# Single transposes and another order in the memory stage of an encoder block

## The chip, the cores and the metric

The kernel runs on one core of one Trainium2 chip. The metric is the device time of one execution in microseconds (us), and the time before is the median of three runs. The core has a matrix engine (TensorE: PE for its products, PEld for its weight loads), a vector engine (DVE), a scalar engine (ACT), GpSimd (POOL), and a sync engine (SP) that issues transfers here. Each engine works through its own list of instructions in order and waits for the others by semaphores.

## The reference

One layer of a residual block on 256 rows (T) of 1024 columns (D), in float32:

```python
x = x + 0.5 * rmsnorm(swiglu(rmsnorm(x), ffn1_w_in, ffn1_w_down))       # FFN 1, width 2816
h = rmsnorm(x)
q_a, f_a, i_a, g_a, q_b, k_b, v_b, f_b, gates = split(h @ w_in)
o_a = rmsnorm(hgrn2(q_a, f_a, i_a)) * silu(g_a)                         # gated recurrence, 8 heads
o_b = fox_attention(q_b, k_b, v_b, f_b)                                 # causal attention, 8 heads
y = sigmoid(gate_a) * (o_a @ w_branch_a) + sigmoid(gate_b) * (o_b @ w_branch_b)
x = x + rmsnorm(y @ w_out)
# the memory stage: 4 heads of 256, 256 rows of memory
q = rmsnorm(x) @ w_mq
k, v = split(rmsnorm(mem) @ w_mkv)
x = x + rmsnorm((softmax(q @ k.T / 16) @ v) @ w_mo)
x = x + 0.5 * rmsnorm(swiglu(rmsnorm(x), ffn2_w_in, ffn2_w_down))       # FFN 2
```

All norms have gains of their own.

## The kernel before

**Numbers as pairs.** Every float32 operand of a product is held as a high part (rounded to the float32r format by an ACT copy) and a low part (what is left, by a DVE subtraction). `split` makes such a pair, `gain_split` makes it with a norm's gain multiplied in, `Pair` holds one for a transposed 1024 x 256 activation. A product of two pairs is three TensorE products: high by high, high by low, low by high.

**Weights.** `unit` brings one weight block of 128 x 1024 (512 KB, 260 in all): a transfer to `raw`, the ACT copy to `hi` (L119) and the DVE subtraction to `lo` (L120). There are buffers for four raw blocks and eight pairs. `chunk` is four units.

**Two kinds of projection.** `proj_tok` has the activations stationary and 512 weight columns moving: rows on partitions in the result. `proj_col` has the weights stationary and 256 rows moving: a transposed result. Each takes eight contraction blocks (kb) of three products.

**Halves and transposes.** The 256 rows are worked on as two halves h of 128. After each sublayer `post` takes the norm of a half from the accumulators (two squares on ACT, a chain of small DVE steps for the reciprocal root, `rstd_of`) and adds it to the residual `xs` (L296, two instructions of 512 columns). Then `half` transposes that half for the next sublayer: `to_T` issues eight TensorE transposes of 128 x 128, four to a bank of `trp` (two banks), and a `gain_split` of each block into X1 to X4. `half` also starts the next reciprocal root, r1 to r4. In the FFN that begins with its first columns row by row (FFN 2: `n_tok` = 2), `act_T` transposes 128 x 256 activations in pairs.

**Order of the work.** The instructions are written down in program order, and a planner with a cost model puts each engine's list into order: of what it takes to be ready, the earliest in the program goes first. The list of products is kept in `log`. `after(i)` gives the instructions inside it high priority, and those on TensorE may not stand ahead of product `log[i]`. This is a lower bound: if the planner takes the operands to be ready later, they stand later. The constants say how many products after a mark (`m`, `n`, or before the end of `log` for `L_OA`): `L_F1` for X2's first half, counted from the last products of FFN 1; `L_IA` for X2's second half, in the projection `i_a`; `L_OA` for OA, the recurrence's output; `L_WO` and `L_MK` for X3 (the memory stage's queries); `L_MO` and `L_F2` for X4 (FFN 2); `L_ACT` and `L_ACT2` for `act_T`.

**The memory stage (L796 to L904).** `rows_proj` with `w_out` ends in accumulators `po[h]`. In program order there follow keys (`mk`, two chunks, 96 products each of 256 columns), queries (`mq`, the same, from X3), values 0 (`mem_v(0)`, 48 products of 512 columns), then for each half the scores (24 products of 256 columns) and the softmax (a maximum per head on DVE, four exponentials on ACT, the normalization L863) and eight transposes of p (L867) with their splits into `pT`; then values 1, and `mem_out(0)` to `mem_out(3)`, 12 products of 256 columns for each of the four heads, which need `pT` and the values, and whose results in the `trp` banks are split into AO; last the projection `mo` from AO.

Of the kernel before, what the change touches and what calls it, by code (L numbers as in the profile page):

```python
# [16 lines left out]
P = 128  # L17
D = 1024
T = 256
# [9 lines left out]

L_ACT = 15  # L30
L_ACT2 = 27
L_F1 = 18
L_IA = 22
L_WO = 18
L_MK = 46
L_MO = 18
L_F2 = 44
L_OA = 20
F_T = (10, 50)
F_O = (30, 75)  # L40
M_O = (24, 36)

R_AT = (12, 30, 48, 68, 88, 120, 160, 193, 218)

# [19 lines left out]
def block_kernel(ctx: ExitStack, tc: tile.TileContext, wts, x_in, xT_in, mem_in, memT_in, cols, rows, fbias, masks, out):  # L64
# [193 lines left out]
    def gain_split(X, kb, src, g, a=0, b=T):  # L258
        gs = cols_s[:, g + kb : g + kb + 1]
        S.activation(X.hi(kb, a, b), src, AF.Copy, scale=gs)  # L260
        V.scalar_tensor_tensor(out=X.lo(kb, a, b), in0=src, scalar=gs, in1=X.hi(kb, a, b).bitcast(F32), op0=ALU.mult, op1=ALU.subtract)  # L261

    def to_T(X, src, h, g):

        for q in range(2):
            ps = trp()
            for j in range(4):
                kb = 4 * q + j
                PE.transpose(ps[:, j * P : (j + 1) * P], src(kb), ident)  # L269
# [31 lines left out]
    def ffn(w_in, w_dn, X, r2, row, n_tok, i_row, first_half, second_half=None):  # L301
        acts = {}

        def scale_row(z, ps):
            if isinstance(ps, list):
                for i in range(2):
                    V.tensor_tensor(out=z[:, i], in0=ps[i], in1=row, op=ALU.mult)
            else:
                V.tensor_tensor(out=z, in0=ps, in1=bc(row, [P, 2, T], 1), op=ALU.mult)  # L309

        def act_tok(c, h):
            ps = mm()
# [4 lines left out]
            V.scalar_tensor_tensor(out=a, in0=ps[:, FC:], scalar=r2[h], in1=sg, op0=ALU.mult, op1=ALU.mult)  # L317
            return a

        def act_T(a, h, act):  # L320
            tr = trp()
            for j in range(2):
                PE.transpose(tr[:, j * P : (j + 1) * P], a[:, j * P : (j + 1) * P], ident)
            split(act[:, 0, :, h * P : (h + 1) * P], act[:, 1, :, h * P : (h + 1) * P], tr[:, :FC].rearrange("p (j t) -> p j t", j=2))

        def act_col(c, act, first=None):
            u = chunk(w_in, c)
            if first:
                pg, pu = proj_first(X, u, first)
            else:  # L330
                pg = proj_col2(X, u, (0, 1))
            z = m4([P, 2, 2, T], n="z")
            scale_row(z[:, 0], pg)
            S.activation(z[:, 0], z[:, 0], AF.Silu)  # L334
            if not first:
                pu = proj_col2(X, u, (2, 3))
            scale_row(z[:, 1], pu)
            V.tensor_tensor(out=z[:, 0], in0=z[:, 0], in1=z[:, 1], op=ALU.mult)
            split(act[:, 0], act[:, 1], z[:, 0])

        def down(c, h):
            act = acts[c]
            hs = slice(h * P, (h + 1) * P)
            for j in range(2):
                wh, wl = unit(w_dn, 2 * c + j)
                ah, al = act[:, 0, j, hs], act[:, 1, j, hs]
                for n in range(2):
                    ns = slice(n * 512, (n + 1) * 512)
                    for i, (a, w) in enumerate(((ah, wh), (ah, wl), (al, wh))):
                        MM(accs[h][n], a, w[:, ns], start=(c == 0 and j == 0 and i == 0), stop=(c == NFF - 1 and j == 1 and i == 2))  # L350

        late = None
        for c in range(n_tok):
            acts[c] = m4([P, 2, 2, T], F32R, "act")
        for h in range(2):
            m = len(log)
            for c in range(n_tok):
                n = len(log)
                ev = act_tok(c, h)
                if late:  # L360
                    with after(n + L_ACT):
                        late()
                late = (lambda ev=ev, c=c, h=h: act_T(ev, h, acts[c]))
            if h == 0 and n_tok:
                second_half(m)
        accs = None
        done = 0
        if callable(row):
            row = row()
        for c in range(n_tok, NFF):  # L370
            acts[c] = m4([P, 2, 2, T], F32R, "act")
            n = len(log)
            act_col(c, acts[c], {0: [acc] * 4, 1: [mm, mm, trp, trp]}.get(c))
            if late:
                with after(n + L_ACT2):
                    late()
# [50 lines left out]

    def half(X, r, h, g, m):

        with after(m):  # L430
            to_T(X, x_blocks(h), h, g)
        r[h] = rstd_x(x_halves(h))

    ffn("f1_in", "f1_dn", X1, r1, row1, 0, 0, lambda m: half(X2, r2, 0, G_MIX, m + L_F1))
# [294 lines left out]
            S.activation(t[:, h, :], ps, AF.Copy, scale=r2[h])  # L729
        vb_.append(t)  # L730
    for h in range(2):
        with after(len(log) - L_OA * (2 - h)):
            to_T(OA, lambda kb: Gt[kb // 4][:, h, (kb % 4) * P : (kb % 4 + 1) * P], h, G_HG)


    zs = []
# [75 lines left out]
    for c in range(2):  # L812
        u = chunk("mk", c)
        KM.more()
        for j in range(2):
            js = slice(2 * j, 2 * j + 2)
            ps = proj_col2(M, u, (2 * j, 2 * j + 1))
            t = sp.tile([P, 2, T], F32, tag="z2", name=nm("km"), bufs=3)
            V.tensor_tensor(out=t, in0=ps, in1=bc(rowm, [P, 2, T], 1), op=ALU.mult)
            split(KM.h[c][:, js], KM.l[c][:, js], t)  # L820
        if c == 0:
            half(X3, r3, 1, G_MEM, m + L_MK)
    for c in range(2):
        u = chunk("mq", c)
        QM.more()
        for j in range(2):
            js = slice(2 * j, 2 * j + 2)
            ps = proj_col2(X3, u, (2 * j, 2 * j + 1))
            split(QM.h[c][:, js], QM.l[c][:, js], ps)

    def mem_v(c):
        u = chunk("mv", c)
        VM.more()
        for h in range(2):
# [7 lines left out]
    mem_v(0)  # L842
    pT = Pair()
    for h in range(2):
        a, b = h * P, (h + 1) * P
        sc = s1(name="sc")
        V.tensor_scalar(out=sc, in0=r3[h], scalar1=1.0 / 16.0, scalar2=None, op0=ALU.mult)
        pv = score_psum()
        for i in range(4):
            for j in range(2):  # L850
                kb = 2 * i + j
                MM(pv[i], QM.hi(kb, a, b), KM.hi(kb), start=(j == 0), stop=False)
                MM(pv[i], QM.hi(kb, a, b), KM.lo(kb), start=False, stop=False)
                MM(pv[i], QM.lo(kb, a, b), KM.hi(kb), start=False, stop=(j == 1))
        mx, sm = s1(4, name="mx"), s1(4, name="sm")
        for i in range(4):
            V.tensor_reduce(out=mx[:, i : i + 1], in_=pv[i], axis=AX.X, op=ALU.max, negate=True)
# [3 lines left out]
            S.activation(p[:, i], pv[i], AF.Exp, bias=mx[:, i : i + 1], scale=sc, accum_out=sm[:, i : i + 1])  # L861
        V.reciprocal(sm, sm)
        V.tensor_tensor(out=p, in0=p, in1=bc(sm, [P, 4, T], 2), op=ALU.mult)  # L863
        for sb in range(2):
            tr = trp()
            for i in range(4):
                PE.transpose(tr[:, i * P : (i + 1) * P], p[:, i, sb * P : (sb + 1) * P], ident)  # L867
# [19 lines left out]
    m = len(log)  # L887
# [102 lines left out]
```

## Time and profile before

| | |
|---|---|
| median of three runs | 815.56 us (814.79 to 817.03) |
| the profiled execution | 814.88 us |
| its span, first to last instruction | 813.1 us |
| granted TensorE clock | 0.998 |
| instructions in the span | 15302 |
| bytes moved | 147.02 MB, mean 181 GB/s |
| weight blocks, issue to landing | 4.5 us median, 260 of 512 KB |

The times of single instructions are from the one profiled execution. The span is what the profile covers; the rest of the execution's time lies around it. A TensorE instruction's length in the profile includes its passage through the array, so instructions that follow each other overlap: what a product costs the stream is the distance from its start to the next start.

Where the work stands in that execution: FFN 1 ends and `i_a` begins at 196.8 us; `i_a` is followed from 221 us by the other projections; `w_out` begins at 486.6, keys at 508.8, values 0 at 557.3, scores at 568.2, values 1 at 574.0, `mo` at 589.8, FFN 2 at 616.0.

### The profile page before, as it was taken

The numbers are of one execution on the slowest core, as the hardware profiler recorded it, in microseconds if no ns is written. First come the engines' busy times: TensorE is split into PE (matmuls) and PEld (weight loads), VectorE is DVE, ScalarE is ACT, GpSimd is POOL, SyncE is SP. The second block draws the span as 40 slices with busy tenths as digits, with TensorE's granted clock in tenths as the row PEclk, the third lists the DMA queues.
The fourth block names the chain that finished last, engine by engine and source line by source line (L and its number), as shares of the span: only waits on it lengthen the run. The fifth ranks groups of instructions, "written<-read, shape, count | busy, mean of one in ns | idle before, by whom it ended". The sixth has DMA issues, their size and how long they took to land.

```text
span 813.1 us, 15302 instructions
## 1 busy us (share of the span) xinstructions
PE 799.4 (98%) x6292; PEld 743.5 (91%) x6292; DVE 538.7 (66%) x866; ACT 409.7 (50%) x621; POOL 10.2 (1%) x22
## 2 busy tenths in 40 slices
PE   8999999999999999999999999999999999999996
PEld 8999999997799889998999998999887899999994
DVE  6964666468776896678585556975748654665454
ACT  7644544436664435348675335744647544444431
POOL 0000000000000100100000000000000000000000
PEclk9999999999999999999999999999999999999999
DMA  8874466464564454543477446456426664566421
GB/s 322 256 264 156 163 207 226 157 207 160 171 208 170 149 193 161 198 152 121 139 231 243 150 168 220 156 179 203 143 83 197 208 207 156 164 212 227 149 104 52
DMA packets 41093, 147.02 MB, mean 181 GB/s; under 512 B 4744, under 2 KB 4752, under 8 KB 41024
## 3 DMA queue, kind: packets, MB, share of 16 engines
q1 hardware_dynamic: 40320, 144.20, 52.3%
q0 software_dynamic: 560, 1.81, 0.7%
q8 instruction: 49, 0.80, 0.4%
q14 instruction: 20, 0.16, 0.1%
q10 hardware_dynamic: 144, 0.04, 0.0%
HBM read 144.97 MB, written 1.06 MB: 180 GB/s over the span
## 4 chain that ended last, share of the span: by engine, by line
PE 92%; DVE 4%; DMA 2%; issue 1%; ACT 1%; DVEq 0%; ACTq 0%
PE mm L78 66%; PE acc L78 22%; PE tr L78 2%; DVE lo L120 1%; DMA raw<-in_wts_dram 1%; DVE xs L296 1%; PE tr L269 1%; ACT junk L235 1%; DVE t L224 1%; DMA cols_s<-in_cols_dram 0%; DVE y L226 0%; DVE post L292 0%; PE tr L697 0%; ACT hT L260 0%; PE tr L867 0%
## 5 line engine op out<-in xcount | busy, mean ns | idle before, releaser
L120 DVE TENSOR_TENSOR lo<-raw,hi 128x1024 fp32r<-128x1024 f32 (+1 forms) x262 | 315.5, 1221 | 134.3 <-ACT hi L119 131.8
L78 PE MATMUL mm<-hT,hi 128*128 128x256 f32 x1240 | 351.3, 283 | 0.0
L78 PE MATMUL mm<-lT,hi 128*128 128x256 f32 x1240 | 351.2, 283 | 0.0
L78 PE MATMUL mm<-hT,lo 128*128 128x256 f32 x1240 | 351.1, 283 | 0.0
L119 ACT CAST hi<-raw 128x1024 fp32r<-128x1024 f32 (+1 forms) x262 | 263.5, 1045 | 132.8 <-PE mm L78 87.9
L78 PEld LDWEIGHTS mm<-lT,hi 128*128 128x128 f32 x1240 | 237.9, 192 | 0.7
L78 PEld LDWEIGHTS mm<-hT,hi 128*128 128x128 f32 x1240 | 237.9, 192 | 0.6
L78 PEld LDWEIGHTS mm<-hT,lo 128*128 128x128 f32 x1240 | 237.8, 192 | 0.1
L78 PE MATMUL acc<-hi,act 128*128 128x512 f32 x352 | 111.4, 390 | 0.0
L78 PEld LDWEIGHTS acc<-hi,act 128*128 128x128 f32 x352 | 66.2, 188 | 13.4
L78 PE MATMUL acc<-lo,act 128*128 128x512 f32 x176 | 68.7, 390 | 0.0
L78 PE MATMUL mm<-hi,hT 128*128 128x512 f32 x160 | 63.1, 395 | 0.0
L78 PE MATMUL mm<-hi,lT 128*128 128x512 f32 x160 | 63.0, 394 | 0.0
L78 PE MATMUL mm<-lo,hT 128*128 128x512 f32 x160 | 62.8, 394 | 0.0
L309 DVE TENSOR_TENSOR z<-mm,row 128x512 f32<-128x512 f32 x36 | 24.8, 689 | 39.0 <-PE mm L78 39.0
L334 ACT ACTIVATE z<-z 128x512 f32<-128x512 f32 x20 | 12.6, 631 | 73.5 <-DVE z L309 73.4
L78 PEld LDWEIGHTS acc<-lo,act 128*128 128x128 f32 x176 | 33.1, 188 | 6.2
L78 PEld LDWEIGHTS mm<-hi,hT 128*128 128x128 f32 x160 | 30.1, 188 | 6.5 <-ACT hT L260 0.7
L78 PEld LDWEIGHTS mm<-hi,lT 128*128 128x128 f32 x160 | 30.1, 188 | 6.4 <-DVE lT L261 0.3
L78 PEld LDWEIGHTS mm<-lo,hT 128*128 128x128 f32 x160 | 30.1, 188 | 5.8
L292 DVE SCALAR_TENSOR_TENSOR post<-acc,grow 128x512 f32<-128x512 f32 x16 | 11.0, 690 | 30.1 <-ACT junk L235 29.6
L235 ACT ACTIVATE junk<-acc 128x512 f32<-128x512 f32 x20 | 12.0, 600 | 35.9 <-PE acc L78 35.6
(195 smaller groups left out, 703.4 us busy)
## 6 DMA issues: line engine op xcount, KB each, us to landing
raw<-in_wts_dram SPq DMA_DIRECT2D x260, 512.0 KB, 4.5
grow<-in_rows_dram SPq DMA_DIRECT2D x4, 512.0 KB, 5.9
xT<-in_xT_dram SPq DMA_DIRECT2D x4, 256.0 KB, 5.5
xs<-in_x_dram SPq DMA_DIRECT2D x2, 512.0 KB, 7.8
cbm<-cd POOLq DMA_DIRECT2D x2, 512.0 KB, 6.6
memT<-in_memT_dram SPq DMA_DIRECT2D x2, 512.0 KB, 6.9
ms<-in_mem_dram SPq DMA_DIRECT2D x2, 512.0 KB, 6.5
out_dram<-xs SPq DMA_DIRECT2D x4, 256.0 KB, 2.0
```

Source lines behind the costliest of these rows:

```text
L78: log.append(PE.matmul(*args, **kw).ins)
L119: S.copy(hi[:, cut], raw[:, cut])
L120: V.tensor_tensor(out=lo[:, cut], in0=raw[:, cut], in1=hi[:, cut].bitcast(F32), op=ALU.subtract)
L224: V.scalar_tensor_tensor(out=t, in0=v, scalar=y, in1=y, op0=ALU.mult, op1=ALU.mult)
L235: S.activation(junk[:, : src.shape[-1]], src, AF.Square, accum_out=dst)
L269: PE.transpose(ps[:, j * P : (j + 1) * P], src(kb), ident)
L292: V.scalar_tensor_tensor(out=t, in0=ps[j], scalar=-factor / 256.0, in1=grow[:, j * 512 : (j + 1) * 512], op0=ALU.mult, op1=ALU.mult)
L296: V.scalar_tensor_tensor(out=xh, in0=t, scalar=r, in1=xh, op0=ALU.mult, op1=ALU.add)
L309: V.tensor_tensor(out=z, in0=ps, in1=bc(row, [P, 2, T], 1), op=ALU.mult)
L334: S.activation(z[:, 0], z[:, 0], AF.Silu)
```

## The change

`to_T` and `act_T` no longer stand as a whole behind one product. Each transpose has a bound of its own: the transpose of block kb stands behind product m + kb, so that one product can lie between two transposes. The splits keep high priority. `half` passes the mark on, and the constants are set anew: `L_F1` 18 to 27, `L_IA` 22 to 40, `L_MO` 18 to 26; X3's two halves get `L_MV`.

In the memory stage values 0 come first, and X3's two halves are put into them (marks 4 and 36); then keys, queries, the scores of both halves together by chunk (heads 0 and 1 for both halves, then heads 2 and 3), the softmax of both, then values 1. The transposes of p had no bound and get one in values 1 (`L_PM`: marks 24 and 40, one product after the other). `mem_out` 0 and 1, which had bounds in values 1 (`M_O`), have none now. `post` of the second half of `w_out` comes ahead of X3's first half in the program.

```diff
 L_ACT = 15
 L_ACT2 = 27
-L_F1 = 18
-L_IA = 22
-L_WO = 18
-L_MK = 46
-L_MO = 18
+L_F1 = 27
+L_IA = 40
+L_MV = (4, 36)
+L_PM = (24, 40)
+L_MO = 26
 L_F2 = 44
 L_OA = 20
...
-M_O = (24, 36)
...
-    def to_T(X, src, h, g):
+    def to_T(X, src, h, g, m):
         for q in range(2):
             ps = trp()
             for j in range(4):
                 kb = 4 * q + j
-                PE.transpose(ps[:, j * P : (j + 1) * P], src(kb), ident)
-            for j in range(4):
-                gain_split(X, 4 * q + j, ps[:, j * P : (j + 1) * P], g, h * P, h * P + P)
+                with after(m + kb):
+                    PE.transpose(ps[:, j * P : (j + 1) * P], src(kb), ident)
+            with tc.high_priority():
+                for j in range(4):
+                    gain_split(X, 4 * q + j, ps[:, j * P : (j + 1) * P], g, h * P, h * P + P)
...
-        def act_T(a, h, act):
+        def act_T(a, h, act, m):
             tr = trp()
             for j in range(2):
-                PE.transpose(tr[:, j * P : (j + 1) * P], a[:, j * P : (j + 1) * P], ident)
-            split(act[:, 0, :, h * P : (h + 1) * P], ...)
+                with after(m + j):
+                    PE.transpose(tr[:, j * P : (j + 1) * P], a[:, j * P : (j + 1) * P], ident)
+            with tc.high_priority():
+                split(act[:, 0, :, h * P : (h + 1) * P], ...)
...
     def half(X, r, h, g, m):
-        with after(m):
-            to_T(X, x_blocks(h), h, g)
+        to_T(X, x_blocks(h), h, g, m)
         r[h] = rstd_x(x_halves(h))
...
     post(po[0], 0, g2)
-    m = len(log)
     rows_proj(po[1], Y, "w_out", 1, range(4, 8))
-    half(X3, r3, 0, G_MEM, m + L_WO)
     post(po[1], 1, g2)
...
+    m = len(log)
     mem_v(0)
+    half(X3, r3, 0, G_MEM, m + L_MV[0])
+    half(X3, r3, 1, G_MEM, m + L_MV[1])
+    for c in range(2):
+        u = chunk("mk", c)
...
+    for c in range(2):
+        u = chunk("mq", c)
...
+    pvs = [score_psum() for _ in range(2)]
+    for c in range(2):
+        for h in range(2):
+            a, b = h * P, (h + 1) * P
+            for i in (2 * c, 2 * c + 1):
+                for j in range(2):
+                    kb = 2 * i + j
+                    MM(pvs[h][i], QM.hi(kb, a, b), KM.hi(kb), start=(j == 0), stop=False)
+                    MM(pvs[h][i], QM.hi(kb, a, b), KM.lo(kb), start=False, stop=False)
+                    MM(pvs[h][i], QM.lo(kb, a, b), KM.hi(kb), start=False, stop=(j == 1))
...
+        ps_m.append(p)
+    m = len(log)
+    mem_v(1)
+    for h in range(2):
+        a, b = h * P, (h + 1) * P
         for sb in range(2):
             tr = trp()
             for i in range(4):
-                PE.transpose(tr[:, i * P : (i + 1) * P], p[:, i, sb * P : (sb + 1) * P], ident)
-            split(pT.h[sb][:, :, a:b], pT.l[sb][:, :, a:b], tr.rearrange("p (i s) -> p i s", i=4))
+                with after(m + L_PM[h] + 4 * sb + i):
+                    PE.transpose(tr[:, i * P : (i + 1) * P], ps_m[h][:, i, sb * P : (sb + 1) * P], ident)
+            with tc.high_priority():
+                split(pT.h[sb][:, :, a:b], pT.l[sb][:, :, a:b], tr.rearrange("p (i s) -> p i s", i=4))
...
-    m = len(log)
-    mem_v(1)
-    for i in range(2):
-        with after(m + M_O[i]):
-            mem_out(i)
-    for i in range(2, 4):
+    for i in range(4):
         mem_out(i)
```

More of the change, by code (lines that the diff above doesn't have):

```diff
@@ L318, in act_tok @@
             return a
-        def act_T(a, h, act):
+        def act_T(a, h, act, m):
             tr = trp()
             for j in range(2):
-                PE.transpose(tr[:, j * P : (j + 1) * P], a[:, j * P : (j + 1) * P], ident)
-            split(act[:, 0, :, h * P : (h + 1) * P], act[:, 1, :, h * P : (h + 1) * P], tr[:, :FC].rearrange("p (j t) -> p j t", j=2))
+                with after(m + j):
+                    PE.transpose(tr[:, j * P : (j + 1) * P], a[:, j * P : (j + 1) * P], ident)
+            with tc.high_priority():
+                split(act[:, 0, :, h * P : (h + 1) * P], act[:, 1, :, h * P : (h + 1) * P], tr[:, :FC].rearrange("p (j t) -> p j t", j=2))
         def act_col(c, act, first=None):
@@ L360, in ffn @@
                 if late:
-                    with after(n + L_ACT):
-                        late()
-                late = (lambda ev=ev, c=c, h=h: act_T(ev, h, acts[c]))
+                    late(n + L_ACT)
+                late = (lambda m, ev=ev, c=c, h=h: act_T(ev, h, acts[c], m))
             if h == 0 and n_tok:
@@ L374, in ffn @@
             if late:
-                with after(n + L_ACT2):
-                    late()
+                late(n + L_ACT2)
                 late = None
@@ L731, in block_kernel @@
     for h in range(2):
-        with after(len(log) - L_OA * (2 - h)):
-            to_T(OA, lambda kb: Gt[kb // 4][:, h, (kb % 4) * P : (kb % 4 + 1) * P], h, G_HG)
+        to_T(OA, lambda kb: Gt[kb // 4][:, h, (kb % 4) * P : (kb % 4 + 1) * P], h, G_HG, len(log) - L_OA * (2 - h))
     zs = []
@@ L803, in block_kernel @@
     post(po[0], 0, g2)
-    m = len(log)
     rows_proj(po[1], Y, "w_out", 1, range(4, 8))
-    half(X3, r3, 0, G_MEM, m + L_WO)
     post(po[1], 1, g2)
     KM, QM, VM = Pair(0), Pair(0), Pair(0)
-    m = len(log)
[L812 to L829, printed above, removed]
     def mem_v(c):
@@ L840, in mem_v @@
             V.scalar_tensor_tensor(out=vl, in0=ps, scalar=rm[h], in1=vh.bitcast(F32), op0=ALU.mult, op1=ALU.subtract)
+    m = len(log)
     mem_v(0)
+    half(X3, r3, 0, G_MEM, m + L_MV[0])
+    half(X3, r3, 1, G_MEM, m + L_MV[1])
+    for c in range(2):
+        u = chunk("mk", c)
+        KM.more()
+        for j in range(2):
+            js = slice(2 * j, 2 * j + 2)
+            ps = proj_col2(M, u, (2 * j, 2 * j + 1))
+            t = sp.tile([P, 2, T], F32, tag="z2", name=nm("km"), bufs=3)
+            V.tensor_tensor(out=t, in0=ps, in1=bc(rowm, [P, 2, T], 1), op=ALU.mult)
+            split(KM.h[c][:, js], KM.l[c][:, js], t)
+    for c in range(2):
+        u = chunk("mq", c)
+        QM.more()
+        for j in range(2):
+            js = slice(2 * j, 2 * j + 2)
+            ps = proj_col2(X3, u, (2 * j, 2 * j + 1))
+            split(QM.h[c][:, js], QM.l[c][:, js], ps)
+    pvs = [score_psum() for _ in range(2)]
[3 more added lines that the diff above has]
+            for i in (2 * c, 2 * c + 1):
+                for j in range(2):
+                    kb = 2 * i + j
+                    MM(pvs[h][i], QM.hi(kb, a, b), KM.hi(kb), start=(j == 0), stop=False)
+                    MM(pvs[h][i], QM.hi(kb, a, b), KM.lo(kb), start=False, stop=False)
+                    MM(pvs[h][i], QM.lo(kb, a, b), KM.hi(kb), start=False, stop=(j == 1))
     pT = Pair()
+    ps_m = []
     for h in range(2):
-        a, b = h * P, (h + 1) * P
+        pv = pvs[h]
         sc = s1(name="sc")
         V.tensor_scalar(out=sc, in0=r3[h], scalar1=1.0 / 16.0, scalar2=None, op0=ALU.mult)
[L848 to L854, printed above, removed]
         mx, sm = s1(4, name="mx"), s1(4, name="sm")
```

1 line of the change is left out of this document (removed).

## The prediction

> **What bounds the kernel now.** I read the shares of the page, then the chain of waits, then what TensorE waited for, then its timeline around each place the change touches, and there the starts of single instructions.
>
> The page, first the busy time of each engine, then the chain that ended last:
>
> ```profile
> PE 799.4 (98%) x6292; PEld 743.5 (91%) x6292; DVE 538.7 (66%) x866; ACT 409.7 (50%) x621; POOL 10.2 (1%) x22
> ...
> PE 92%; DVE 4%; DMA 2%; issue 1%; ACT 1%; DVEq 0%; ACTq 0%
> ```
>
> TensorE is the bound nearly everywhere. No product is added or removed, so the change acts in two ways only: what a transpose costs in the TensorE stream, and TensorE's idle stretches. The waits of TensorE, longest sum first (us in total, times, longest):
>
> ```profile
> PE acc L78 <- ACT hi L119: 2.4, 1, 2.4
> PE tr L269 <- DVE xs L296: 1.1, 2, 0.9
> PE tr L78 <- DVE ones L195: 1.1, 1, 1.1
> PE tr L323 <- DVE at L317: 0.5, 1, 0.5
> PE tr L269 <- issue: 0.2, 1, 0.2
> ```
>
> The first and third are the start of the kernel, which is not touched. The others are transposes waiting for the residual row block (L296) or the FFN activation (L317). The view counts idle time only after a product's modelled end, so I take the loss from starts: a 512-wide product follows another by 0.227 us, a 256-wide one by 0.120. What a step takes beyond that is the loss. TensorE's timeline at four places (start, length, instruction):
>
> ```profile
> 190.32 0.39 PE L78 MATMUL acc<-lo,act 128*128 128x512 f32 x1
> 190.91 0.63 PE L269 MATMUL tr<-ident,xs 128*128 128x128 f32 x4 [0.20 <-issue]
> 191.29 0.48 PE L78 MATMUL acc<-hi,act 128*128 128x512 f32 x1
> 191.61 0.60 PE L269 MATMUL tr<-ident,xs 128*128 128x128 f32 x4
> 191.97 0.48 PE L78 MATMUL acc<-hi,act 128*128 128x512 f32 x1
> 192.28 0.39 PE L78 MATMUL acc<-lo,act 128*128 128x512 f32 x1
> ...
> 205.82 0.39 PE L78 MATMUL mm<-hi,lT 128*128 128x512 f32 x1
> 207.08 1.32 PE L269 MATMUL tr<-ident,xs 128*128 128x128 f32 x8 [0.86 <-DVE xs L296]
> ...
> 583.50 0.39 PE L78 MATMUL mm<-hi,lT 128*128 128x512 f32 x1
> 583.73 1.03 PE L867 MATMUL tr<-ident,pm 128*128 128x128 f32 x8
> 584.52 0.48 PE L78 MATMUL mm<-hi,hT 128*128 128x512 f32 x1
> 584.83 0.39 PE L78 MATMUL mm<-lo,hT 128*128 128x512 f32 x1
> ...
> 589.32 0.40 PE L78 MATMUL mm<-hi,lT 128*128 128x512 f32 x1
> 589.81 0.50 PE L78 MATMUL acc<-hi,hT 128*128 128x512 f32 x1
> ```
>
> Loss at each place, in us, from the starts:
> - X2 first half (190.3): 0.39. X2 second half (205.8): 1.30, of it 1.02 before the first transpose and 0.28 among the eight.
> - The first products of `i_a` (198.65): 0.36, for the gain splits of X2.
> - X3: 0.52 at 509.2 and 0.16 at 521.2.
> - First `mo` product (589.3): 0.36, for the split of AO.
> - X4 first half (609.4): 0.44. The first `act_T` and X4's second half (625.7 to 628.6): 0.92.
>
> Together 4.45 us: the most that better placing can bring.
>
> **The transposes themselves.** In the run of eight at 583.73 one follows another by (1.03 - 0.27)/7 = 0.109 us. The stream loses 0.90 us to the whole run, the slightly longer steps of the five products behind it included. A single transpose between two 512-wide products isn't in this trace, but nearly: between the two fours at 190.91 and 191.61 stands one product. From the last transpose of the first four (191.26) to the first of the second (191.61) is 0.35 us for one transpose and one product: 0.35 - 0.227 = 0.12. At 610.4 the same comes to 0.11 to 0.12. So eight singles cost 8 x 0.12 plus the tail of 0.02, 0.98 us: 0.08 to 0.10 more than a run of eight. In the 256-wide stream a single costs 0.113, no more than in a run. Seven runs (two of X2, one of OA, two of p, two of X4) give 7 x 0.09 = 0.6. X3's two move from the 256-wide stream, where they cost 0.87 without stalls, to the 512-wide one: 2 x 0.12 = 0.2. The four pairs of `act_T` add 0.05. Sum +0.85, bounds +0.3 (many still fall together) and +1.1.
>
> The row of L269 gives 0.273 us for one transpose from start to end. The Trainium skill (TensorE: Matmul & The Clock Gate, Part 4: PE-mode transpose) puts a transpose at about 275 ns in a kernel, mostly access latency. The trace agrees on the length (273), but 0.12 is what the stream loses. By the page's figure taken as the full price, 80 singles would cost some 13 us more, an estimate; the sum does not use it.
>
> **Places of the transposes.** The constant is only a lower bound: where the data come later in the planner's reckoning, the transposes stand later. X2's first half has the bound 18, but 22 of the last 48 products follow it, so it stands behind 26; the second half has 22 and stands behind 39.
> - X2 first half, new bound 27: behind 28, so 0.45 us later. That covers the 0.36 before the first transpose. Gain 0.39.
> - X2 second half, 40: behind 41, 0.45 later, of 1.02. The other half of the row, 0.67 us later (L296 twice in 1.41), is hidden by the products between. Gain 1.30 - 0.57 = 0.73.
> - X4 first half, 26: one product later, and spread. Gain 0.24.
> - OA's second half stands today at 387.7, long after its bound, so all eight may still go together: 0.
> - `act_T` and X4's second half: the 0.67 before L323 is `at`, which stands on DVE behind both L296 of the second half. Neither moves. Gain 0.1 from the spreading, of 0.92.
>
> **The memory stage.** Values 0 (48 products, 10.9 us) now come first, with X3's transposes in them. The first half stands behind five 512-wide products: 508.81 + 5 x 0.227 = 509.95, and L296 delivers at 509.53 and 510.19, so it does not wait. For the second half, `post` of h=1 now precedes X3's reciprocal root in the program. Today that root holds DVE from 515.6 to 518.7 and only then h=1 goes on, to 521.8. Without it h=1 should be ready near 517, and the bound (37 products, eight transposes) is 508.81 + 8.4 + 1.0 = 518.2. Gain 0.68. X3 is read by the queries 23 us later. Values 0 take their four weight blocks past the sixteen of keys and queries on SP's queue and through the casts. Each group of four serves about 11 us of products either way (48 x 0.227 or 96 x 0.120), against 4.5 us to landing and 4 x 1.22 on DVE: cost 0, covered by the eight buffers that `w_out` frees in the same order.
>
> The scores lose their cover: values 0 stood between queries and scores. The last query split is needed after 30 score products, 3.6 us; it takes 0.62 + 0.69 plus a weight cast (1.05 ACT, 1.22 DVE) ahead of each at worst, 3.6. Cost 0, at most 0.3. The softmax is covered by values 1: p of h=0 was ready at 576.55, 5.5 us after its scores; here it has 1.4 + 5.7 = 7.1 us. p of h=1 has 10.3 us, and takes two maxima, four exponentials behind those of h=0, a reciprocal and L863: about 8. Cost 0, at most 1.
>
> The new wait is at the end of values 1. The last of p's transposes stands behind the 48th product, and behind it TensorE has only `mem_out`, which needs the split of that bank. From 584.36 to 586.45 today's two splits show: copy 0.59, subtraction 0.69; for h=0 the last low part was ready 1.8 us after the start of the last transpose (578.83 to 580.62), and the second copy alone would make it 1.65. On ACT the eviction of values 1 (L839, 0.71) is ready just before the copy and goes first, up to 0.9 after that start: low part at 2.2 us. Meanwhile there are ten products without it, from 0.11 to 1.31. Wait 2.2 - 1.31 = 0.9, bounds 0.35 (no eviction ahead) and 1.95 (a weight cast of 1.05 ahead on ACT). Behind it `mem_out` 2 and 3 wait for their banks, filled by `mo` products as today: 0.25. Today's 0.36 goes. Cost 0.90 + 0.25 - 0.36 = +0.79.
>
> Last, spreading eight transposes over 2.5 us instead of 1.3 lets the gain splits of X2 and X4 start up to 1.2 us later. Today their last low parts come 0.36 late at `i_a` and 0.2 before need at the second FFN. I take +0.2, bounds -0.3 and +2.2.
>
> **Sum.** Gains 0.39 + 0.73 + 0.24 + 0.10 + 0.68 = 2.14. Costs 0.85 + 0.79 + 0.20 = 1.84. Net -0.3 us: span 813.1 becomes 812.8, the profiled execution of 814.88 (span and 1.8 around it) becomes 814.6. That run stood 0.68 below the median of the three shown, 815.56; beside the median I forecast 815.3.
>
> **Rivals.**
> 1. Faster: the row blocks also come earlier. The chains to L296 hold weight casts of 1.22 between their small steps, two before X2's second half; sorted elsewhere, all transpose stalls vanish. Then 0.39 + 1.30 + 0.68 + 0.44 + 0.92 = 3.73, less 0.85: -2.9, 812.7. For it: the order on DVE shifts with every moved split. Against: none of these casts is itself moved.
> 2. Slower: ACT takes the copies out of the spread transposes late, behind weight casts that wait for a buffer. Today one did: the cast at 197.72 had waited 1.49 with three of X2's splits behind it. Price: 1.2 at `i_a`, 1.0 at the second FFN, 1.05 at `mem_out`, less 0.2 counted: +3.05 on -0.3, 818.3. It decides once splits slip over 0.2 us. Against: they keep high priority.
> 3. The points don't bind: data come later than every bound and the transposes fall together. Only the memory stage counts: 0.79 - 0.68, 815.7. For it: today's places lie 4 to 17 products behind the bounds. Against: the new bounds lie behind today's places.
> 4. A lone transpose pays its whole 0.273, so 80 x (0.273 - 0.109) = +13 us, 828. Against: 0.12 around 191.29. The Trainium skill's figure for a transpose (same section) would lead there.
>
> **How the numbers follow.** 0.3%, about 2.4 us, is what a measurement can tell from no change. Forecast 0.40 (its own range 813.6 to 817.4: the bounds of its terms, of which not all fall alike), rival 1 0.25, rival 2 0.23, rival 3 0.10, rival 4 0.02. Faster 0.25, same 0.50, slower 0.25. The range reaches to rivals 1 and 2 with a little beyond, 812.2 to 818.6.
>
> **What would show it.** Right: single transposes stepping 0.35 with a product, in place of x8 rows; the wait before L269 at X2's second half about 0.5; none at X3; a gap of about 0.8 between the last p transpose and the products of `mem_out`. Wrong: p transposes that wait for L863, gain splits arriving over 1 us after `i_a` or the second FFN starts, or the 0.9 us at the second FFN gone.

## The result: slower by 0.26%, where a gain of 0.3 us was forecast

Changed kernel: median 817.48 us (816.14 to 819.10); kernel before in the same session: 815.04 us (814.12 to 817.03). Ratio 1.0026, 95% interval 1.0020 to 1.0033, so 1.6 to 2.7 us lost. The forecast was 815.3 against a median of 815.56, no change that can be told. 817.48 lies inside the range, and 0.26% just under the 0.3% that the text took for the least a measurement can tell; but the interval excludes no change, and the sign was not the forecast's.

The page of the profile after shows the busy time of each engine, then the shares of the chain that ended last:

```profile
PE 800.4 (98%) x6292; PEld 742.2 (91%) x6292; DVE 539.8 (66%) x866; ACT 410.0 (50%) x621; POOL 9.9 (1%) x22
...
PE 92%; DVE 3%; ACT 2%; DMA 2%; issue 1%; DVEq 0%; ACTq 0%
```

TensorE has as many instructions as before and 1.0 us more busy time; the span is 815.0 against 813.1. Now the waits of TensorE (us in total, times, longest):

```profile
PE acc L77 <- ACT hi L118: 2.5, 1, 2.5
PE mm L77 <- ACT hT L259: 1.5, 3, 1.1
PE tr L77 <- DVE lT L133: 1.3, 2, 0.9
```

The first is the start, as before. What the change was to shorten is gone: no transpose waits for the row block (L298 now) or for the activation. The other two lines are new in their place, 2.8 us together: projections that wait for a gain split's high part on ACT (L259), and `mem_out` waiting for a low part of p's split on DVE (L133). The waits did not go away, they moved from the transposes to the splits behind them.

By stage, from starts of the first instructions on TensorE, in us. The second line ends where the row of X2's reciprocal roots (`row2`) is built, behind the last product of `i_a`; the expectations call this point the second row:

```
stage                                            before   after   diff
start to i_a (holds X2's first half)             195.77   195.58  -0.19
i_a to its second row (X2's second half)          24.37    24.70  +0.33
from there to memory (not touched but for OA)    287.60   287.69  +0.09
memory to first score (X3)                        59.39    58.82  -0.57
scores                                             5.75     5.76  +0.01
values 1 to second FFN (p, mem_out, mo, X4)       42.03    43.31  +1.28
second FFN to its first down product              36.76    37.69  +0.93
rest                                             160.36   160.35  -0.01
```

The sum is +1.9. Stretches that no edit touches are not equal in the profiles below: the first 30 us differ by up to 1.25 between two of them, the third line of the table by up to 1.6. So spans are not compared below; stages and timed ratios are.

Three places on TensorE after (start, length, instruction):

```profile
191.15 0.27 PE L270 MATMUL tr<-ident,xs 128*128 128x128 f32 x1
191.18 0.48 PE L77 MATMUL acc<-lo,act 128*128 128x512 f32 x1
191.50 0.27 PE L270 MATMUL tr<-ident,xs 128*128 128x128 f32 x1
...
198.46 0.39 PE L77 MATMUL mm<-hi,lT 128*128 128x512 f32 x1
199.91 0.50 PE L77 MATMUL mm<-hi,hT 128*128 128x512 f32 x1 [1.06 <-ACT hT L259]
...
207.29 0.27 PE L270 MATMUL tr<-ident,xs 128*128 128x128 f32 x1
...
586.31 0.27 PE L878 MATMUL tr<-ident,pm 128*128 128x128 f32 x1
587.44 0.38 PE L77 MATMUL tr<-hT,hT 128*128 128x256 f32 x1 [0.86 <-DVE lT L133]
587.66 0.28 PE L77 MATMUL tr<-hT,lT 128*128 128x256 f32 x1
587.78 0.28 PE L77 MATMUL tr<-lT,hT 128*128 128x256 f32 x1
587.90 0.28 PE L77 MATMUL tr<-hT,hT 128*128 128x256 f32 x1
588.02 0.28 PE L77 MATMUL tr<-hT,lT 128*128 128x256 f32 x1
588.70 0.39 PE L77 MATMUL tr<-lT,hT 128*128 128x256 f32 x1 [0.40 <-DVE lT L133]
```

The first rows are single transposes: 0.35 from one to the next, 0.12 above a product's step, as the prediction worked out. At 198.46 a projection of `i_a` waits: 199.91 - 198.46 - 0.23 = 1.22 us lost. At 207.29 X2's second half starts 0.23 behind the product ahead of it (207.06), where 1.02 us were lost before. At the end of values 1 the first product of `mem_out` starts 1.13 behind the last transpose (1.02 of it lost), and after five products a second wait loses 0.56.

Why the split is late is on ACT's timeline, first of after, then of before:

```profile
197.70 1.05 ACT L118 CAST hi<-raw 128x1024 fp32r<-128x1024 f32 x1 [1.27 <-DMA raw<-in_wts_dram]
198.66 0.58 ACT L234 ACTIVATE junk<-acc 128x512 f32<-128x512 f32 x1
...
199.24 0.61 ACT L259 ACTIVATE hT<-tr,cols_s 128x128 fp32r<-128x128 f32 x2
```

```profile
197.72 1.05 ACT L119 CAST hi<-raw 128x1024 fp32r<-128x1024 f32 x1 [1.49 <-DMA raw<-in_wts_dram]
198.68 0.62 ACT L260 ACTIVATE hT<-tr,cols_s 128x128 fp32r<-128x128 f32 x2
199.18 0.60 ACT L235 ACTIVATE junk<-acc 128x512 f32<-128x512 f32 x1
```

In both, a weight cast waits long for its transfer (1.27 and 1.49), ends near 198.75, and two gain splits stand behind it. Before, they follow at once, the needed one first: done at 199.04, and the product started at 199.09. After, a square of FFN 1's sums (L234, 0.58) goes ahead of them, and the needed one is second (199.49 to 199.85; the product at 199.91): 0.58 + 0.25 = 0.83 later, for a product that is due 0.19 earlier. That is the growth of the wait, from 0.21 to 1.22. Its transpose was done by 192.5, so what held the split was its place behind the cast.

### The profile page after: what moved, and what is told of

Its sections match the earlier page's. It is cut to its first block, busy times and chain, and to the rows that moved or that the text cites. A ratio compares the mean times of both kernels' runs of the same rounds, so it can differ in the third digit from the quotient of the medians.

```text
span 815.0 us, 15306 instructions
## 1 busy us (share of the span) xinstructions
PE 800.4 (98%) x6292; PEld 742.2 (91%) x6292; DVE 539.8 (66%) x866; ACT 410.0 (50%) x621; POOL 9.9 (1%) x22
## 4 chain that ended last, share of the span: by engine, by line
PE 92%; DVE 3%; ACT 2%; DMA 2%; issue 1%; DVEq 0%; ACTq 0%
PE mm L77 67%; PE acc L77 23%; PE tr L77 2%; DMA raw<-in_wts_dram 1%; DVE lo L119 1%; ACT junk L234 1%; DVE xs L298 1%; PE tr L270 0%; ACT hT L259 0%; DMA cols_s<-in_cols_dram 0%; DVE t L223 0%; PE tr L698 0%; ACT hi L118 0%; DVE post L294 0%; DVE y L225 0%
## 5 line engine op out<-in xcount | busy, mean ns | idle before, releaser
L234 ACT ACTIVATE junk<-acc 128x512 f32<-128x512 f32 x20 | 11.9, 596 | 36.9 <-PE acc L77 36.7
```

The costliest lines, as they stand in the source:

```text
L234: S.activation(junk[:, : src.shape[-1]], src, AF.Square, accum_out=dst)
```

## The experiments

Times are read against the kernel before in the same session; intervals are 95%. Which part costs what came first.

**e1: transposes in runs.** The memory stage and all bounds are as after, but the transposes of X2, OA, X3, X4 and the activations stand in runs (p's stay single). The splits now lie inside `after`, which gives them the same high priority as in before and after:

```diff
-        for q in range(2):
-            ps = trp()
-            for j in range(4):
-                kb = 4 * q + j
-                with after(m + kb):
+        with after(m):
+            for q in range(2):
+                ps = trp()
+                for j in range(4):
+                    kb = 4 * q + j
                     PE.transpose(ps[:, j * P : (j + 1) * P], src(kb), ident)
-            with tc.high_priority():
                 for j in range(4):
                     gain_split(...)
```
and the same in `act_T`.

> The changed kernel with the transposes of to_T and act_T in runs again, all eight (or two) behind product m with the new constants; the memory stage stays as changed, and p's transposes stay single. Theory (spreading makes the gain splits late, and the first products of i_a and FFN 2 wait for them): the wait of 1.2 us at i_a falls to about 0.4, but the wait of X2's second half for L296 comes back with about 0.6; the waits of 1.6 us at FFN 2 fall to about 0.9; five and a half runs cost 0.09 us less each. About 1.6 us less than the changed kernel: near 815.9 us. Rival (only the price of the transposes in the stream counts): 0.5 us less, near 817.0.

Measured: 1.0003 (0.9994 to 1.0012), 1.9 us below after; the theory had 1.6, the rival 0.5. In the profile the wait in `i_a` is 0.24, and X2's second half waits 0.60 for its row block.

**e2: the old memory stage.** After, with the memory stage of before:

```diff
-L_MV = (4, 36)
-L_PM = (24, 40)
+L_WO = 18
+L_MK = 46
+M_O = (24, 36)
... (memory stage as before)
```

> The changed kernel with the memory stage of before (keys, queries, values 0, scores, values 1 with mem_out 0 and 1 in it), X3's halves at their old marks; single transposes and new constants elsewhere. Theory (the end of values 1 costs 1.5 us more than before, X3 gives 0.6 back): about 0.9 us less than the changed kernel, near 816.6 us, so about 1.5 above before from X2 and FFN 2 alone. Rival (the memory stage is a gain, as the waits at X3 suggest, and all the loss is in the single transposes): 0.6 us more than the changed kernel, near 818.1.

Measured: 1.0011 (1.0003 to 1.0020): the theory's -0.9 would give 1.0015 and the rival's +0.6 1.0033, so the rival falls. Its second FFN still takes 37.85: with the old order too, the single transposes and the later bound of X4 cost 1.1 there.

**e9: the new memory stage alone.** e1 with the bounds of before:

```diff
-L_F1 = 27
-L_IA = 40
+L_F1 = 18
+L_IA = 22
-L_MO = 26
+L_MO = 18
```

> Only the memory stage is as after (values first, then keys, queries, scores, second values, p's transposes one by one at 24 and 40); everywhere else the transposes stand in runs and the lower bounds of X2 and X4 are those of before. Theory (the order of the memory stage by itself costs the second FFN something, because casts and transfers meet the splits of X4 in another phase): first FFN with i_a as before (220.1 to 220.6 us), keys to scores 58.8 (before 59.39), values 1 to second FFN 43.2 to 43.4 (before 42.03), second FFN to its first down product 37.4 to 37.9 (before 36.76); ratio 1.0020. Rival (the second FFN pays only for spread transposes and late bounds): second FFN 36.7 to 36.9, ratio 1.0009.

Measured: 1.0016 (1.0006 to 1.0026); stages 24.12, 58.84, 43.48 and 37.38. The second FFN is 0.62 over before without one spread transpose in it, at the edge of what the theory expected and away from the rival: the wait before the first activation's transpose (`at`) is 0.95 here, 0.67 before. So 1.3 us belong to the memory stage's order and 0.9 to the transposes and their bounds with the old order (e2); 2.2 together, and 2.1 was measured for both. The parts add, as far as intervals of 0.8 us to each side can tell.

**e7: the bounds.** After, single transposes and all, with the three bounds of before as in e9:

> The changed kernel with L_F1, L_IA and L_MO at their old values (18, 22, 18): to_T still issues one by one, but the marks lie ahead of the data, so X2's two halves and X4's first half fall into runs at the places of before. Theory (the form costs nothing where the marks do not bind; what is left is the memory stage, 1.3 us lost behind values 1 less 0.6 won at X3, and 0.3 for the single transposes there): i_a as before (a wait of 1.0 for L296, 0.4 for the splits), FFN 2 0.3 us longer than before, in all 1.0 to 1.3 us above before, a ratio of 1.0014. Rival (the marks do not matter, single issue does): 1.0026 as the changed kernel.

Measured: 1.0019 (1.0009 to 1.0029): both fit, so the ratio settles nothing. With those bounds X2's transposes and those of X4's first half fall together again, and the stage of `i_a` is back at 24.08 with a wait of 0.8 for the row block. But the second FFN takes 38.18, 1.4 over before where 0.3 was expected. TensorE waits there 0.75 for a split behind a cast that had waited 1.80 for its transfer, 0.73 for `at`, and 0.44 behind the transposes of X4's second half, which are still partly spread. So a late split at the second FFN needs no spread first half.

**e3, e4, e8, e5: the end of values 1 and the second FFN.** In e3 p's transposes come earlier; e4 has the edits of e1 as well:

```diff
-L_PM = (24, 40)
+L_PM = (18, 30)
```

> The changed kernel with L_PM = (18, 30) for (24, 40), nothing else: p's last transposes stand behind product 42 of values 1, so six products (1.4 us) lie between them and mem_out. Theory (the 1.6 us behind values 1 are the split of the last bank without cover): the two waits of 1.02 and 0.56 us fall to about 0.3 together, 1.2 us less than the changed kernel, near 816.3 us. Rival (the wait only moves: to p's transposes, which then wait for the softmax, or to the banks of mem_out 2 and 3): the same as the changed kernel, 817.3 to 817.7.

> Both edits: to_T and act_T in runs, and L_PM = (18, 30). Theory (independent places on one engine's chain, so they add): 1.6 + 1.2 = 2.8 us less than the changed kernel, near 814.7 us, level with before or up to 0.5 us under it: the order of the memory stage itself then pays its 0.6 at X3. Rival (a wait taken away at one place comes back at the next, since the vector and scalar engine set the pace there): less than 2 us gained, above 815.5.

Measured: e3 1.0013 (1.0005 to 1.0022), 1.1 us below after; e4 0.9995 (0.9986 to 1.0005), 2.5 below. In the times the edits add, at the sizes expected. But the two waits of e3, expected at 0.3 together, are still one of 0.93, with six 512-wide products behind the last transpose, and the stage is only 0.7 shorter than after's. DVE's timeline in e3 says why:

```profile
584.29 1.22 DVE L119 TENSOR_TENSOR lo<-raw,hi 128x1024 fp32r<-128x1024 f32 x1
585.42 0.69 DVE L133 TENSOR_TENSOR lT<-tr,hT 128x512 fp32r<-128x512 f32 x1
586.03 1.22 DVE L119 TENSOR_TENSOR lo<-raw,hi 128x1024 fp32r<-128x1024 f32 x1
587.16 0.68 DVE L133 TENSOR_TENSOR lT<-tr,hT 128x512 fp32r<-128x512 f32 x1
```

A weight subtraction of 1.22 stands ahead of each of the two subtractions of p. e8 takes such subtractions away; it leaves out the low part of `mo`'s weights, the high part standing in:

```diff
-    lo = wp.tile([P, D], F32R, tag="lo", ...)
+    lo = wp.tile([P, D], F32R, tag="lo", ...) if low else hi
...
-    wh, wl = unit(name, kb)
+    wh, wl = unit(name, kb, low=name != "mo")
```

> The changed kernel without the low parts of the mo weights: their eight DVE subtractions of 1.22 us are left out and the high part is used in their place, so TensorE does the same products on other numbers. Theory (behind values 1 the low parts of p stand on DVE behind weight subtractions of mo, and the copy on ACT behind the eviction L818): the first wait falls from 1.02 to about 0.2, the second stays near 0.5; 0.8 to 0.9 us less than the changed kernel there, a ratio of 1.0015. Rival (the wait is the eviction and the copy on ACT alone): both waits as they are, 1.0024 to 1.0028.

Measured: 1.0028 (1.0018 to 1.0039), as after, so the gain that the theory expected did not come. TensorE's timeline of e8 at the end of values 1:

```profile
586.60 0.39 PE L77 MATMUL tr<-hT,hT 128*128 128x256 f32 x1 [0.21 <-DVE lT L134]
...
587.53 0.38 PE L77 MATMUL tr<-hT,hT 128*128 128x256 f32 x1 [0.31 <-ACT hT L133]
...
588.44 0.39 PE L77 MATMUL tr<-lT,hT 128*128 128x256 f32 x1 [0.41 <-DVE lT L134]
```

The wait at the first product fell from 1.02 to 0.37, but three products on a wait of 0.47 for the second bank's copy has come (the eviction of values 1, L819 there, goes ahead of that copy on ACT), and 0.56 for its subtraction stays: 1.40 in sum, 1.58 after. The weight subtraction sets the first wait only; the second bank's copy and subtraction set the end.

e5 is e4 with X4's old bound, L_MO = 18:

> The kernel with runs of transposes and L_PM = (18, 30), and L_MO back from 26 to 18. The mark does not bind then: X4's first half stands behind 26 and 27 products of mo, as before, not behind 28. FFN 2's stretch up to its first down product took 36.8 us before, 37.7 changed, and still 37.4 and 37.8 with runs. Theory (the later mark, not the spreading, makes X4's splits slip behind a weight cast, and with them the chain to the first act_T): the stretch falls to about 36.9, and the kernel by 0.8 us, to a ratio of 0.9985 to before. Rival (the stretch is longer for another reason, the new order ahead of it): 37.6 or more, and a ratio of 0.9995 as without this edit.

Measured: 1.0004 (0.9992 to 1.0015), second FFN 37.68 with 1.25 before `at`. The bound is not why the second FFN is longer here; the rival held.

**e11 to e15: is it the spreading?** e11 gathers X2's transposes alone, still at high priority:

```diff
-                with after(m + kb):
+                with after(m if g == G_MIX else m + kb):
```

> After, but X2's two halves stand as runs of eight at the same bounds (28 and 41 products), their splits still at high priority; all other transposes one by one, memory stage as after. Theory (the single transposes of X2 make a gain split of i_a late behind a weight cast on ACT): the wait of 1.22 us in the first products of i_a falls to at most 0.3, a wait of about 0.6 before X2's second half comes back, stage i_a to its second row 23.9 to 24.1 (after 24.70), ratio 1.0017 to 1.0021. Rival (the late split comes from the later place of X2's first half or from the priority of the splits, not from the spreading): the wait in i_a stays near 1.2, with 0.6 more before the second half, stage 25.2, ratio 1.0032.

Measured: 1.0024 (1.0015 to 1.0034), which holds both readings. The stage fell further than expected, to 23.31, with no wait in `i_a`, yet the time hardly moved. Either the priority of the splits or a wait that differs between executions had to explain that, so four kernels stood side by side. e14 is after itself, e15 is e1 itself. e13 is after with ordinary priority for the splits of `to_T` and `act_T`. e12 is e1 with `high_priority` written around these splits too. The expectations say that e15 lacks the raised priority; it does not, because `after` already gives it, and e12 raises that of `to_T`'s splits a second time.

> All bounds and the memory stage as after; the transposes of X2, OA, X3, X4 and of the activations in runs, but their splits still at high priority. Theory A (the spreading costs: eight single transposes lose 0.1 us more than a run, and hold back a split): as e15, 1.9 us below e14, ratio 1.0003. Theory B (the raised priority costs: a split taken early on ACT and DVE displaces weight casts and the steps of post): as e14, ratio 1.0026.

> After with its single transposes, but the splits of to_T and act_T without the raised priority (p's splits keep it). Theory A: as e14, ratio 1.0026, at worst slower. Theory B: as e15, ratio 1.0003.

> The changed kernel again, unaltered: ratio 1.0026. If the wait of 1.22 us in i_a belongs to the program, this profile shows it again at product 9 of i_a and a stage of 24.6 to 24.8; if it belongs to one execution (a weight block that landed late), the stage is 23.3 to 24.1 here.

> The kernel of e1 again, unaltered (transposes of X2, OA, X3, X4 and of the activations in runs, no raised priority, everything else as after): ratio 1.0003, i_a to its second row 23.9 to 24.1, second FFN 37.3 to 37.5, if these are the program's; another split of the same total if single executions differ by more than 0.3 in a stage.

```
                      ratio (interval)            start to i_a   i_a stage   sum      2nd FFN
e14 single, high      1.0024 (1.0015 to 1.0033)   196.15         24.04       220.19   38.38
e13 single, ordinary  1.0026 (1.0013 to 1.0040)   196.03         24.96       220.99   37.83
e12 runs, high twice  1.0008 (0.9999 to 1.0016)   196.08         23.78       219.86   36.97
e15 runs, high        1.0005 (0.9995 to 1.0014)   195.74         23.71       219.45   37.17
(after, first run)    1.0026 (1.0020 to 1.0033)   195.58         24.70       220.28   37.69
(e11)                 1.0024 (1.0015 to 1.0034)   196.46         23.31       219.77   37.81
```

Theory A holds: the spreading costs, and the priority nothing that can be seen. The medians of the two single kernels lie 1.2 to 2.1 us above those of the two with runs; e14 and e15, at the same priority, are 1.7 apart. In the profiles, from singles to runs, the mean up to `i_a`'s second row falls from 220.5 (after, e14, e13) to 219.8 (e1 with 220.00, e12, e15), the second FFN from 38.0 to 37.2: 1.5 us together. Two profiles of one program differ by as much as 0.7 in these stages, and in e4 and e5, also in runs, the second FFN takes 37.76 and 37.68. So the 1.5 fits the times, but its split over the two stages is not shown.

The sums and the transfers clear up e11. Its `i_a` began 0.88 later than in the first profile of after, 0.65 of it from the first 30 us, which no edit touches. The cast on ACT that `i_a` waits behind hangs on a transfer, and began at nearly the same time in three profiles: 197.58 in e11, 197.63 in e14 and 197.70 in after. The transfer was issued at 193.44, 193.34 and 192.79, later by about as much as `i_a`, but took 4.06, 4.21 and 4.84 us to land. So e14, the same program as after, lost 0.58 there instead of 1.22, and the sums agree to 0.1. A late start alone does not help: in e13 `i_a` began 0.46 later than in after, the transfer took 5.01, and 1.14 were lost. In sums e11 gains 0.5 of the 1.4 that its stage showed, which its times (0.2, within about 1) allow.

The order on ACT does not differ between profiles of one program. In every profile with X2's first half spread (after, e14, e13, e3, e8, e2) a square stands between this cast and the two splits, at either priority; in all others, e11 and e12 among them, the splits follow the cast at once. ACT in e11, to be held against the lines of after above:

```profile
197.58 1.05 ACT L118 CAST hi<-raw 128x1024 fp32r<-128x1024 f32 x1 [0.87 <-DMA raw<-in_wts_dram]
198.54 0.61 ACT L259 ACTIVATE hT<-tr,cols_s 128x128 fp32r<-128x128 f32 x2
199.05 0.59 ACT L234 ACTIVATE junk<-acc 128x512 f32<-128x512 f32 x1
```

So the spreading sets the order, and the landing sets how much of it TensorE pays. Runs are not safe either: in e5 the transfer took 5.32, and the split still cost 0.75.

Where the splits are not late the old waits are back. TensorE's waits in e14, then in e15:

```profile
PE mm L77 <- ACT hT L259: 1.4, 3, 0.7
```

```profile
PE tr L325 <- DVE at L318: 1.0, 1, 1.0
...
PE tr L270 <- DVE xs L297: 0.4, 1, 0.4
```

**e6, e10: towards a faster version.** e6 has runs, the old memory stage with X3 later (behind products 9 and 92 of the keys, and behind `post` of the second half in the program), `L_F1` = 27, `L_IA` = 40, `L_MO` = 18. e10 has the same bounds for X2 and X4, with values 0 and X3 ahead of the keys, and the rest of the memory stage as before.

> Runs of transposes, L_F1 = 27 and L_IA = 40 as changed, L_MO = 18 as before, the memory stage in the order of before, but post of the second half ahead of X3 in the program and X3's halves behind products 9 and 92 of the keys. No part of the change's spreading and none of its order. Theory (the waits of X2 and X3 are a matter of the mark alone, and values 0 and mem_out keep their cover): FFN 1 with i_a 1 us shorter than before, keys to scores 0.6 us shorter, values 1 and FFN 2 as before: 1.5 us under before, a ratio of 0.998. Rival (what is won at X2 and X3 is lost at the next wait): 0.9993 to 1.0003.

> Transposes in runs, bounds 27 and 40 for X2 and 18 for X4; of the memory stage's new order only its first half: values 0 with X3's transposes ahead of the keys and queries, but scores, softmax, p's transposes and the products of mem_out as before. Theory (the gain of X3 and the loss at the end of values 1 are separate parts): i_a to its second row 23.5 to 24.0 (before 24.37), keys to scores 58.8, values 1 to second FFN 42.0, and the second FFN 36.8 if its loss belongs to the new order of softmax and mem_out; ratio 0.9980. Rival (the second FFN pays for values 0 standing ahead of the keys, since this shifts every later weight block): second FFN 37.7, ratio 0.9993. A third reading (p's second half now has only values 1 as cover behind scores of its own head) would show as a wait for the softmax multiplication before p's transposes.

Measured: e6 0.9998 (0.9987 to 1.0010), e10 1.0005 (0.9995 to 1.0014). e6's four stages (23.86, 59.07, 42.01, 36.74) are 0.87 shorter than before's, with 0.3 of the 0.6 hoped for at X3; the time shows no gain, as the rival had it. In e10 values 1 to second FFN take 43.13: p's second half now stands three products from the end, and 0.60 + 0.72 are lost there and at `mo`'s first product. Its second FFN, 37.07, lies between theory and rival. Nothing tried, e4 included, is measurably faster than before.

## Why the prediction was wrong

- **Price of a single transpose: right.** Among p's transposes a transpose and a product take 0.345, so 0.12 for the transpose, against 0.109 in a run. By the figure of the Trainium skill (TensorE: Matmul & The Clock Gate, Part 4: PE-mode transpose), about 275 ns, taken as full price, e14 would lie some 7 us above e12 (over 40 spread transposes at 0.166 more each, an estimate); it lies 1.2 above. The trace agrees with that figure as a length (0.27), not as what the stream loses. Rival 4 is out.
- **X2: the first half right, the second not as described.** The first half no longer waits: its first transpose at 191.15 follows in step. For the second half the forecast put the loss that stays at 0.57. With runs it is 0.57 in e15, 0.60 in e1 and 0.31 in e12, so the agreement is partly luck. In after it is nought, because `i_a` had already stood 1.2 us for a split: the gain of 1.30 was paid for earlier.
- **X3: right.** 0.68 less its share of singles; the stage gave 0.57. The reason fits: no transpose waits, and the second half's row block was ready at 516.9 (forecast near 517; 521.8 before), though its transposes stood in fours in the keys.
- **"Spreading lets the gain splits start later, +0.20": the step that failed first.** It set a small late arrival against 0.36 lost and 0.2 of slack, and kept +2.2 only as a bound; against rival 2 it held that the splits keep high priority. In after the waits for splits are 1.22 and 0.24 in `i_a`, with steps of 0.11 behind them, and 0.32, 0.29, 0.16 and 0.44 in the second FFN. The priority did not keep a square and a waiting cast from standing ahead of them on ACT. Of the 1.5 us between singles and runs, some 0.5 is the transposes (over 40 at about 0.01); the rest, about 1, is left for the late splits, net of the old waits that they hide. Rival 2 had the mechanism, ACT taking the copies late behind weight casts; only the cast waited for the landing of a transfer. Its point, "splits slip over 0.2 us", was reached (0.83). It got a chance of 0.23 though the trace already showed splits behind such a cast.
- **End of values 1, +0.79: mis-sized.** The low part came 2.3 us behind the last transpose (588.64 - 586.31), 2.2 was worked out. But "ten products without it" was wrong: TensorE takes its products in the order of its list, and the sixth of `mem_out` needs that part. Also the first product needs a bank of p's transposes, whose subtraction stood behind a weight subtraction of 1.23 (585.56 to 586.79 on DVE, then 0.68), and the third product needs what that subtraction gives; that wait was left out. Waits 1.02 + 0.56 in place of 0.9 + 0.25. 1.58 less the old 0.36, less 0.24 gained at X4's first half, plus some 0.3 for the singles, is the stage's +1.28. In all profiles with p at these bounds both waits are there and equal within 0.02 us, but for the first in e8.
- **Second FFN: no term for the new order.** e9 shows 0.62 with no spread transposes there. In after `at` ends 10.9 us into the stage, before 10.6. So the wait for it, forecast as nearly unchanged, grows where no split is late, and is hidden in after, where splits are. With runs in the new order the stage takes 36.97 to 37.76 (e12, e15, e1, e9, e5, e4), in the old order 36.76 and 36.74 (before, e6). The weight block issued some 2.8 us ahead of the stage took 4.5 to 6.4 us to land in the new order and 4.0 to 4.9 in the old, but in e9 only 4.88, no more than before's 4.91. So that block alone does not explain it, and the cause stays open.

By terms (us): start to `i_a`'s second row, with X2's stalls gained and its splits late, +0.1 against a forecast of about -0.8; X3 -0.6; values 1 to the second FFN +1.3; second FFN +0.9. 1.9 in the profile, 2.1 in the times.

## What to carry to other kernels

A transpose's place is not where its cost ends: count to the last instruction that its consumers wait for, and look at what stands in order on those engines, above all a cast waiting for a transfer. A sum of several stalls that look removable is an upper bound, since the next wait in each chain is often nearly as late; here the 1.3 us gained at X2's second half had been spent 7 us earlier. For cover behind the last producer, walk the products in the order of the list, and stop at the first that needs either the late data or the late bank.

## What was not expected of the hardware

Two profiles of one program, after and e14, place their waits differently: 1.22 and 0.58 at `i_a`, 0.32 and 0.90 at the first late split of the second FFN. The casts ahead of these splits hang on transfers whose time to landing varies: 4.84 and 4.21 us for the block at `i_a`, 4.31 and 4.88 for the one at the second FFN, each time the longer wait with the slower landing. And TensorE stood idle for a reason that the profile doesn't name ("issue"), in a stretch that no edit touches, in some profiles only. In e6:

```profile
291.74 0.25 PE L77 MATMUL acc<-q,k 128*32 128x16 f32 x7 [1.10 <-issue]
```

In e9 0.37 and 0.81 are lost this way in the same stretch, in before and after nothing. That is more than the effect of most edits here, so a single span could not have judged them.
